# The front of a layer: key norms in pieces and later, bonus products a half later, PSUM banks of their own, three factor steps a block

## The chip, the cores and the metric

The kernel runs on one core of a Trainium2 chip. The metric is the device time of one execution in microseconds (us). TensorE (PE), VectorE (DVE), ScalarE (ACT), GpSimd (POOL) and SyncE (SP, which issues all the DMAs here) each work through their own queue in order and wait for each other by semaphores. PE's loads of weights are listed as PEld.

## What is computed

A block of gated delta rule and dilated attention with its feed-forward net is followed by two layers of a second kind. Each of those projects 1280 tokens (256 of context, 1024 of grid) by a wide matrix and feeds three mixers: a bidirectional RWKV recurrence, grouped-query attention and neighbourhood attention. The change is in the projection for the RWKV part and in the factors that the recurrence takes from it:

```
u = _centred_conv3(u, conv_w)                     # conv over 3 tokens, 1280 channels
r, k, v, dd, ad = split(u)                        # 3 x 384 channels, 2 x 64 of low rank
decay = exp(-exp(-softplus(-(w0 + tanh(dd) @ w2)) - 0.5))      # for two directions
iclr  = sigmoid(a0 + ad @ a2)
kk    = k * k_k, divided by its norm in each head of 64
kd    = k * (1 + (iclr - 1) * k_a)
bonus = sum over a head of (r * (kd_forward + kd_backward) * r_k), times v
```

## The kernel before

`front` (L2318) runs once for each of the two layers, between the block before it and `stage`, where recurrence and attention run. It has three parts, in this order: `project`, `project_att` and `project_na`. A generator, `factors`, is advanced step by step from the first two (`next(side, None)`).

**Order.** In the front, instructions are not placed by hand. The program gives their priority; a scheduler that simulates the engines puts each engine's queue in a fixed order at build time, and an engine that would be idle in this simulation takes later work that is ready. Tiles of one tag share `bufs` slots, and a new tile has to wait until a slot is released. When a pool is closed, the next one takes over its memory, and a tile waits for the tiles that it overlaps. PSUM banks are different: the eight `[128, 512]` banks are single tiles, `K.bank` hands them out by tag and turn (L103), and whoever gets a bank waits, in program order, for the one that had it before. `DENSE` gives banks 0 and 1 to "mm" (dense products), 2 and 3 to "a" (transposes), and 4, 5 and 6 to "r", which norms, transposes of the attention part and factors share. Bank 7 is not used there.

**`project`** (L1377) goes through ten blocks of 128 columns. `Dense.load` brings weights and splits them into a high and a low part; `Dense.chan` (L251) makes, for each of three token segments (256, 512, 512), a chain of 24 products (L243 to L245) into an "mm" bank, and `k.copy` evicts it into `raw`, on ACT (L129) and DVE (L133) in turn. Then the convolution (L1407 to L1409, DVE) writes `cv`. Block 0 holds the hidden layers of the low-rank parts; blocks 1 to 9 are r, k, v of three pairs of heads. Every block is stored in `R`. After a k block (2, 5, 8) follows the key norm: squares into `sq` (L1433, L1434, ACT), sums by `heads_rsqrt_bc` (products L1356, a copy L1358, power of -1/2 on POOL L1361, spread by products L1372), and four multiplications into `kn`, which is the tile of `raw` (L1440), stored by L1444. After a v block (3, 6, 9) ten transposes (L1425) are evicted into `vt` by `k.copy` and stored by twelve small DMAs (L1430). `raw`, `cv` and `sq` share the tag "t5" with four slots. From block 4 on, four steps of `factors` follow each block.

**`factors`** (L1548) treats each of three pairs in two halves of 640 tokens, in five steps a half, 30 in all. A half loads r, k, `kn` and v as one tile `X` (L1567). For each of two directions it makes four small products from the hidden layers (L1577, two for each of two kinds), with tanh evictions on ACT (L1579), then a scan, exponentials and products on DVE, ACT and POOL, and stores `bk` (L1606) and `G` (L1610). At the end `kd` of both directions is summed (L1613, POOL), multiplied (L1614, DVE), summed over a head by PE (L1617) and multiplied into v in place (L1618), which is stored as `vb` (L1619).

**`project_att`** (L1451) makes v for attention token tile by token tile (`nv`, L1464), turns the rest of v, and makes q and k with their norms (`qk_norm`). Its tiles lie in a pool that takes over the memory of `project`'s. `project_na` follows with dense products only.

Of the kernel before, what the change touches and what calls it, by code (L numbers as in the profile page):

```python
# [22 lines left out]
DENSE = {"mm": FULL[0] + FULL[1], "a": FULL[2] + FULL[3], "r": FULL[4] + FULL[5] + FULL[6]}  # L23
FINISH = {"mm": FULL[0] + FULL[1] + FULL[5] + FULL[7], "r": FULL[6] + FULL[2] + FULL[3]}
# [1275 lines left out]
NT = 1280  # L1300
# [77 lines left out]
def project(k, I, l, last, hp, dn, hT, L, side):  # L1378
# [5 lines left out]
    def slot(nm):  # L1384
        return hp.tile([128, 1284], F32, tag="t5", name=nm, bufs=4)


    w = None
    for j in range(10):
# [11 lines left out]
        def ev(p, t0, n):  # L1401
            o = t0 + (1 if t0 < CTX else 3)
            k.copy(raw[:, o:o + n], p)
        dn.chan(w, j % 2 * 128, hT, segs, ev)
        a = slot("cv")
# [9 lines left out]
        else:  # L1415
# [4 lines left out]
            if kind == 2:  # L1420
                for b0, m in ((0, 4), (4, 4), (8, 2)):
                    p = k.bank([128, 4, 128], "a")
                    for i in range(m):
                        o = (b0 + i) * 128 + (0 if b0 + i < 2 else 2)
                        nc.tensor.transpose(p[:, i], a[:, o:o + 128], k.ident)  # L1425
                    vt = hp.tile([128, 2, 4, 64], F32, tag="vt", name="vt", bufs=2)
                    k.copy(vt[:, :, :m], p[:, :m].rearrange("p b (h v) -> p h b v", h=2))
                    for c in range(2):
                        for h in range(2):
                            nc.sync.dma_start(L.vT[:, pr, h, b0 * 2 + c:(b0 + m) * 2:2], vt[c * 64:c * 64 + 64, h, :m])  # L1430
            if kind == 1:
# [3 lines left out]
                kn = raw  # L1435
                for b0, m, p in heads_rsqrt_bc(k, hp, sq, 0, NT, 1.0, "max", 1e-12):

                    for b in ((b0, 2), (b0 + 2, 2)) if b0 == 0 else ((b0, m),):
                        o = b[0] * 128 + (0 if b[0] < 2 else 2)
                        nc.vector.scalar_tensor_tensor(  # L1440
                            kn[:, b[0] * 128:(b[0] + b[1]) * 128].rearrange("p (b t) -> p b t", t=128),
                            a[:, o:o + b[1] * 128].rearrange("p (b t) -> p b t", t=128), L.kk[:, pr:pr + 1],
                            p[:, b[0] - b0:b[0] - b0 + b[1]], ALU.mult, ALU.mult)
                nc.sync.dma_start(L.R[:, pr * 4 + 2, :], kn[:, 0:1280])  # L1444
        if j > 3:
            for _ in range(4):
                next(side, None)

# [98 lines left out]
def factors(k, I, l, wk, L):  # L1547
# [13 lines left out]
    nc.sync.dma_start(hid, L.R[:, 12])  # L1561
    for pr in range(3):
        for a in range(0, NT, N):
            tk = slice(a, a + N)
            pc = slice(pr, pr + 1)
            X = t1("X4", (128, 4, N))
            nc.sync.dma_start(X, L.R[:, pr * 4:pr * 4 + 4, tk])  # L1567
            r, kx, kk, v = (X[:, i] for i in range(4))
            r3, kk3 = (x.rearrange("p (c t) -> p c t", t=64) for x in (r, kk))
            kds = []  # L1570
            for d in range(2):
                th = [t1("th0"), t1("th1")]
                for kind in range(2):
                    for x in range(0, N, 320):
                        p = k.bank([128, 320], "r")
# [4 lines left out]
                                             bias=L.w0[:, kind * 2 + d, pc])  # L1580
                yield
# [33 lines left out]
            for x in range(0, N, 320):  # L1615
                p = k.bank([128, 320], "r")
                nc.tensor.matmul(p, lhsT=k.c("same"), rhs=b[:, x:x + 320], start=True, stop=True)  # L1617
                nc.vector.tensor_tensor(v[:, x:x + 320], v[:, x:x + 320], p, ALU.mult)  # L1618
            nc.sync.dma_start(L.vb[:, pr, tk], v)  # L1619
            yield  # L1620

# [695 lines left out]
def front(k, tc, I, l, last, dn, hT, L, dp):  # L2317

    nc = k.nc
    for nm, shape in (("R", [128, 13, NT]), ("vT", [64, 3, 2, 20, 64]), ("nqk", [128, 4, NT]), ("gqk", [128, 4, NT]),  # L2320
                      ("nv", [128, 10, 384]), ("gates", [128, 8, NT]), ("ydr", [128, 8, NT]), ("bk", [128, 3, 2, 2, NT]),
                      ("G", [128, 3, 2, 20, 128]), ("vb", [128, 3, NT])):
        setattr(L, nm, dp.tile(shape, F32, tag=nm + "d", name=f"{nm}{l}", bufs=1))
    pool = lambda name: tc.tile_pool(name=f"{name}{l}", bufs=1, reuse_waits="tile", side="left")
# [230 lines left out]
```

## Time and profile before

| | us |
|---|---|
| median of three runs | 4414.95 |
| the three runs | 4407.27, 4414.95, 4433.86 |
| the profiled execution | 4414.57 |
| its span | 4412.8 |

The profile is of one execution; its times are counted from the start of the span. The front of layer 0 lies at about 1666 to 2084, that of layer 1 at about 3101 to 3507. "Busy" is time in which an engine executes; matmuls are pipelined, so a row's duration is longer than the distance to the next one. The granted clock of PE is given as a share of 2.4 GHz; 0.5 is 1.2 GHz. Of a row of the timeline, the bracket at its end tells the idle time of the engine just before it and what ended it.

### The profile page before, as it was taken

What the parts mean: (1) busy time and instruction counts of PE and PEld (TensorE: products, weight loads), DVE (VectorE), ACT (ScalarE), POOL (GpSimd) and SP (SyncE); (2) the same over time, 40 slices, a digit from 0 to 9 for tenths busy, and PEclk for the clock granted to TensorE, in tenths of its full rate; (3) what the DMA queues carried; (4) which work ended last, traced back from release to release, by engine and by line L of the source; (5) the groups of instructions that cost most, each with busy time, mean ns of one, the idle gap of its engine ahead of it and who ended that gap; (6) DMA issues with size and microseconds to landing.
All of it is one profiled execution on the core that took longest, in us unless ns stands there. A gap on an engine that the chain in (4) does not pass through costs nothing. (4 is left out here: it accounts for less than half of the span.)

```text
span 4412.8 us, 91628 instructions
## 1 busy us (share of the span) xinstructions
PE 3949.0 (89%) x36914; PEld 3200.0 (73%) x36914; DVE 2166.8 (49%) x4701; ACT 1448.3 (33%) x2831; POOL 1699.5 (39%) x3201
## 2 busy tenths in 40 slices
PE   8989998989999989899869898988989987898878
PEld 6767777967888867578747776778767866676658
DVE  5633332499221155664235555557566424554546
ACT  4244443321111132221125554442222114554341
POOL 2444333433232254342223444336444224434424
PEclk9999999999999989889979999999889998999889
DMA  3343224354111133453232334354345333324434
GB/s 112 117 131 88 82 74 131 127 162 151 44 46 50 43 120 114 152 179 95 81 102 63 74 73 109 91 157 144 114 156 177 104 98 81 76 64 100 100 111 138
DMA packets 523961, 466.87 MB, mean 106 GB/s; under 512 B 66416, under 2 KB 448656, under 8 KB 523408
## 3 DMA queue, kind: packets, MB, share of 16 engines
q1 hardware_dynamic: 523536, 461.02, 35.7%
q8 instruction: 289, 4.73, 0.4%
q14 instruction: 136, 1.11, 0.1%
HBM read 330.43 MB, written 130.43 MB: 104 GB/s over the span
## 5 line engine op out<-in xcount | busy, mean ns | idle before, releaser
L154 POOL TENSOR_TENSOR wlo<-wraw,whi 128x1024 fp32r<-128x1024 f32 (+3 forms) x134 | 318.9, 2395 | 565.1 <-ACT whi L153 513.1
L436 POOL TENSOR_TENSOR wY<-wR,wX 128x60 f32<-128x60 f32 (+5 forms) x900 | 233.3, 259 | 405.2 <-DMA wR<-wD 353.0
L153 ACT CAST whi<-wraw 128x1024 fp32r<-128x1024 f32 (+3 forms) x164 | 156.9, 989 | 372.5 <-PE bank L245 162.8
L691 DVE CUSTOM_DVE_ANT_0 S<-bank,zero 128x256 f32<-128x256 f32 (+1 forms) x372 | 204.5, 558 | 151.4 <-PE bank L687 149.4
L245 PE MATMUL bank<-h2T,wlo 128*128 128x512 f32 x704 | 278.5, 397 | 0.0
L244 PE MATMUL bank<-h2T,whi 128*128 128x512 f32 x704 | 278.0, 395 | 0.0
L243 PE MATMUL bank<-h2T,whi 128*128 128x512 f32 x704 | 275.6, 394 | 0.3 <-ACT h2T L785 0.3
L727 ACT COPY PT<-bank 128x512 f32<-128x512 f32 x346 | 201.7, 584 | 222.4 <-PE bank L723 221.6
L243 PE MATMUL bank<-whi,yh 128*128 128x256 f32 x832 | 240.5, 289 | 31.7 <-ACT yh L153 31.7
L438 POOL TENSOR_TENSOR wX<-wX,wY 128x60 f32<-128x60 f32 (+5 forms) x900 | 239.1, 266 | 70.5
L723 PE MATMUL bank<-cst,S 128*128 128x128 f32 x1416 | 238.4, 292 | 23.5 <-ACT PT L727 14.6
L744 PE MATMUL bank<-PT,nav 128*64 128x128 f32 (+1 forms) x2832 | 242.8, 294 | 16.5 <-ACT PT L727 16.1
L245 PE MATMUL bank<-whi,yl 128*128 128x256 f32 x832 | 238.9, 288 | 0.5 <-POOL yl L154 0.5
L244 PE MATMUL bank<-wlo,yh 128*128 128x256 f32 x832 | 239.2, 288 | 0.0
L744 PEld LDWEIGHTS bank<-PT,nav 128*64 128x64 f32 (+1 forms) x2832 | 154.4, 141 | 86.8 <-issue 55.3
L415 POOL TENSOR_TENSOR wB<-A,cst 128x256 f32<-128x256 f32 x60 | 45.2, 753 | 446.6 <-DVE A L1889 446.5
L723 PEld LDWEIGHTS bank<-cst,S 128*128 128x128 f32 x1416 | 164.1, 146 | 62.8 <-ACT PT L727 26.2
L648 ACT ACTIVATE S<-S,mx 128x1280 f32<-128x1280 f32 (+3 forms) x180 | 202.7, 1127 | 9.1 <-DVE mx L695 6.4
L243 PE MATMUL bank<-hT,whi 128*128 128x512 f32 x464 | 190.4, 410 | 9.1 <-ACT sqkv L131 6.7
L244 PE MATMUL bank<-hT,whi 128*128 128x512 f32 x464 | 187.3, 404 | 0.0
L243 PEld LDWEIGHTS bank<-whi,yh 128*128 128x128 f32 x832 | 162.5, 195 | 33.2 <-ACT yh L153 32.9
L245 PE MATMUL bank<-hT,wlo 128*128 128x512 f32 x464 | 186.2, 402 | 0.0
(467 smaller groups left out, 10919.3 us busy)
## 6 DMA issues: line engine op xcount, KB each, us to landing
wraw<-in_w_in SPq DMA_DIRECT2D x86, 512.0 KB
wR<-wD SPq DMA_DIRECT2D x60, 512.0 KB
wm<-in_w_mod SPq DMA_DIRECT2D x96, 256.0 KB
X<-R SPq DMA_DIRECT2D x12, 1280.0 KB
G<-gt SPq DMA_DIRECT2D x24, 640.0 KB
bk<-bk SPq DMA_DIRECT2D x24, 640.0 KB
bk<-bk SPq DMA_DIRECT2D x120, 128.0 KB
G<-G SPq DMA_DIRECT2D x240, 64.0 KB
```

The source lines that it names most:

```text
L153: self.nc.scalar.copy(hi, raw)
L154: (eng or self.nc.gpsimd).tensor_tensor(lo, raw, hi.bitcast(F32), ALU.subtract)
L243: nc.tensor.matmul(p, lhsT=lh, rhs=rh, start=kk == 0, stop=False)
L244: nc.tensor.matmul(p, lhsT=lh, rhs=rl, start=False, stop=False)
L245: nc.tensor.matmul(p, lhsT=ll, rhs=rh, start=False, stop=kk == n - 1)
L436: eng.tensor_tensor(t, custom(R, i * 64 + i + 1, [((15 - 2 * i) * 64 + 31 - i, 2), (16, 2), (1, n)]), custom(x, i, [(47 - 2 * i, 2), (16, ...
L438: eng.tensor_tensor(o, o, t, ALU.subtract)
L648: nc.scalar.activation(s[:, :total], s[:, :total], AF.Exp, bias=mx[:, 5:6], accum_out=mx[:, 6:7])
L691: nc.vector.tensor_tensor_reduce(out=s[:, c0:c0 + n], in0=p[:, c0 % 512:c0 % 512 + n], in1=b, scale=1.0, scalar=-3.0e38, op0=ALU.add, op1= ...
L723: nc.tensor.transpose(pt[:rows[i], i], P[h][0][:, c0:c0 + rows[i]], k.ident)
L727: nc.scalar.copy(t[:, :full], pt[:, :full])
L744: nc.tensor.matmul(pv[h * 64:h * 64 + 64, 0], lhsT=V, rhs=t[:V.shape[0], i], start=seen[h] == 1, stop=seen[h] == n)
```

## The change

- `front` sets `FRONT`: "mm" and "a" as before, "r" on banks 4 and 5, and a new tag "f" on banks 6 and 7, which all products of `factors` use.
- The tag "t5" has five slots.
- The key norm is a generator, `unit`. Its first `next` comes right after the squares and does nothing; the second comes after the dense products of the next block and does sums, copy and power; the third comes after the dense products of the block after that, or after the loop for block 8, and does the spreading products, the four multiplications and the store. The result goes into `sq` itself, not into `raw`.
- Evictions into `raw` and `vt` are all on ACT.
- Three steps of `factors` follow a block, in place of four.
- In `factors`, v is loaded into a tile `X1` of its own (two slots), the other three into `X3`. The bonus (products, multiplication, store) of a half is kept in `late` and done in the next half, right after the factor products of its first direction; the last one is done at the end.

```diff
+FRONT = {"mm": FULL[0] + FULL[1], "a": FULL[2] + FULL[3], "r": FULL[4] + FULL[5], "f": FULL[6] + FULL[7]}
 ...
-        return hp.tile([128, 1284], F32, tag="t5", name=nm, bufs=4)
+        return hp.tile([128, 1284], F32, tag="t5", name=nm, bufs=5)
+
+    def unit(pr, a, sq):
+
+        yield
+        norms = heads_rsqrt_bc(k, hp, sq, 0, NT, 1.0, "max", 1e-12, slow=True)
+        next(norms)
+        yield
+        for b0, m, p in norms:
+
+            for b in ((b0, 2), (b0 + 2, 2)) if b0 == 0 else ((b0, m),):
+                o = b[0] * 128 + (0 if b[0] < 2 else 2)
+                nc.vector.scalar_tensor_tensor(
+                    sq[:, b[0] * 128:(b[0] + b[1]) * 128].rearrange("p (b t) -> p b t", t=128),
+                    a[:, o:o + b[1] * 128].rearrange("p (b t) -> p b t", t=128), L.kk[:, pr:pr + 1],
+                    p[:, b[0] - b0:b[0] - b0 + b[1]], ALU.mult, ALU.mult)
+        nc.sync.dma_start(L.R[:, pr * 4 + 2, :], sq[:, 0:1280])
 ...
-    w = None
+    w, norm = None, iter(())
     for j in range(10):
 ...
-            k.copy(raw[:, o:o + n], p)
+            nc.scalar.copy(raw[:, o:o + n], p)
         dn.chan(w, j % 2 * 128, hT, segs, ev)
+        next(norm, None)
 ...
-                    k.copy(vt[:, :, :m], p[:, :m].rearrange("p b (h v) -> p h b v", h=2))
+                    nc.scalar.copy(vt[:, :, :m], p[:, :m].rearrange("p b (h v) -> p h b v", h=2))
 ...
-                kn = raw
-                for b0, m, p in heads_rsqrt_bc(k, hp, sq, 0, NT, 1.0, "max", 1e-12):
-                    ...
-                nc.sync.dma_start(L.R[:, pr * 4 + 2, :], kn[:, 0:1280])
+                norm = unit(pr, a, sq)
+                next(norm)
         if j > 3:
-            for _ in range(4):
+            for _ in range(3):
                 next(side, None)
+    next(norm, None)
 ...
+    def bonus(pr, tk, b, v):
+        for x in range(0, N, 320):
+            p = k.bank([128, 320], "f")
+            nc.tensor.matmul(p, lhsT=k.c("same"), rhs=b[:, x:x + 320], start=True, stop=True)
+            nc.vector.tensor_tensor(v[:, x:x + 320], v[:, x:x + 320], p, ALU.mult)
+        nc.sync.dma_start(L.vb[:, pr, tk], v)
+
+    late = None
 ...
-            X = t1("X4", (128, 4, N))
-            nc.sync.dma_start(X, L.R[:, pr * 4:pr * 4 + 4, tk])
-            r, kx, kk, v = (X[:, i] for i in range(4))
+            X, v = t1("X3", (128, 3, N)), t1("X1", bufs=2)
+            nc.sync.dma_start(X, L.R[:, pr * 4:pr * 4 + 3, tk])
+            nc.sync.dma_start(v, L.R[:, pr * 4 + 3, tk])
+            r, kx, kk = (X[:, i] for i in range(3))
 ...
-                        p = k.bank([128, 320], "r")
+                        p = k.bank([128, 320], "f")
 ...
+                if late:
+                    bonus(*late)
+                    late = None
                 yield
 ...
-            for x in range(0, N, 320):
-                ...
-            nc.sync.dma_start(L.vb[:, pr, tk], v)
+            late = pr, tk, b, v
             yield
+    bonus(*late)
 ...
+    k.places = FRONT
```

## Rows read from the trace of the kernel before

**Rows 1.** The page, busy time of each engine and its share of the span.

```profile
PE 3949.0 (89%) x36914; PEld 3200.0 (73%) x36914; DVE 2166.8 (49%) x4701; ACT 1448.3 (33%) x2831; POOL 1699.5 (39%) x3201
```

**Rows 2.** Stretches: length, busy PE, PEld, DVE, ACT, POOL (instructions), PE clock, DMA.

```profile
1666.00:1846.00 180.00, 171.90 (x890) 134.49 (x890) 107.98 (x94) 44.45 (x71) 63.61 (x64) 0.97 0.38 130
1850.70:1894.50 43.80, 23.56 (x99) 15.07 (x100) 27.18 (x31) 13.15 (x23) 25.16 (x16) 0.62 0.55 195
1896.00:2084.00 188.00, 179.49 (x1119) 157.05 (x1119) 100.25 (x127) 42.22 (x71) 69.61 (x85) 0.96 0.41 127
3287.60:3327.80 40.20, 22.91 (x98) 14.98 (x99) 25.57 (x29) 10.30 (x18) 22.47 (x15) 0.63 0.52 185
```

**Rows 3.** Timeline of PE, layer 0: start, us, line, operands, count, idle before.

```profile
1839.84 0.40 PE L244 MATMUL bank<-hA,whi 128*128 128x512 f32 x1
1840.08 0.39 PE L245 MATMUL bank<-hA,wlo 128*128 128x512 f32 x1
...
1850.23 0.28 PE L244 MATMUL bank<-wlo,hA 128*128 128x256 f32 x1
1850.35 0.28 PE L245 MATMUL bank<-whi,hA 128*128 128x256 f32 x1
...
1860.04 2.50 PE L1617 MATMUL bank<-kd,cst 128*128 128x320 f32 x4 [5.66 <-DVE kd L1614]
...
1864.52 4.43 PE L1356 MATMUL bank<-cst,sq 128*128 128x2 f32 x20
...
1894.60 0.88 PE L243 MATMUL bank<-whi,hA 128*128 128x256 f32 x1
```

**Rows 4.** PE's groups in 1850.7 to 1894.5: busy, mean ns, idle before, releaser.

```profile
L1577 PE MATMUL bank<-hid,w2s 32*128 32x320 f32 x22 | 9.9, 606 | 7.1 <-ACT th L1579 7.1
L1617 PE MATMUL bank<-kd,cst 128*128 128x320 f32 x7 | 4.5, 787 | 7.2 <-DVE kd L1614 7.2
...
L1372 PE MATMUL bank<-cst,hrs 128*64 128x128 f32 x40 | 3.8, 375 | 6.1 <-POOL hrs L1361 6.1
```

**Rows 5.** PE's waits, first two layer 0, last layer 1: total, times, longest.

```profile
PE bank L1617 <- DVE kd L1614: 11.0, 4, 5.7
PE bank L243 <- DVE raw L133: 7.1, 2, 5.7
...
PE bank L1356 <- ACT sq L1433: 5.4, 1, 5.4
```

**Rows 6.** Timeline of ACT, layer 0.

```profile
1816.33 0.94 ACT L1579 ACTIVATE th<-bank,w 128x320 f32<-128x320 f32 x2 [5.59 <-DVE bk L1604]
...
1831.53 1.14 ACT L1434 ACTIVATE sq<-cv,kk 128x1024 f32<-128x1024 f32 x1
...
1889.25 0.53 ACT L1579 ACTIVATE th<-bank,w 128x320 f32<-128x320 f32 x1 [2.87 <-DVE bk L1604]
1889.67 0.36 ACT L129 COPY nv<-bank 128x256 f32<-128x256 f32 x1
```

**Rows 7.** Timeline of DVE, layer 0.

```profile
1845.84 0.68 DVE L133 COPY raw<-bank 128x512 f32<-128x512 f32 x1
...
1859.10 0.89 DVE L1614 SCALAR_TENSOR_TENSOR kd<-X,rk,kd 128x640 f32<-128x640 f32 x1 [2.91 <-POOL kd L1613]
...
1869.08 0.88 DVE L1407 TENSOR_SCALAR cv<-raw,conv 128x1282 f32<-128x1282 f32 x1
```

**Rows 8.** Both fronts, by tile: count, then ns min/median/max, first and last start.

```profile
L133 DVE COPY raw<-bank x30: 400/677/692, 1666.4 to 3281.2; 128x512 f32<-128x512 f32 x20, 128x256 f32<-128x256 f32 x10
L129 ACT COPY raw<-bank x27: 351/587/596, 1666.1 to 3273.0; 128x512 f32<-128x512 f32 x20, 128x256 f32<-128x256 f32 x7
...
L1408 DVE SCALAR_TENSOR_TENSOR cv<-raw,conv,cv x20: 1544/1555/3574, 1675.5 to 3302.9; 128x1282 f32<-128x1282 f32 x20
...
L1608 DVE TENSOR_TENSOR gt<-ec,X x24: 809/816/2193, 1744.7 to 3381.3; 128x640 f32<-128x640 f32 x24
```

**Rows 9.** Timeline of SP's queue, layer 0.

```profile
1880.69 7.73 SPq L1430 DMA_DIRECT2D vT<-vt  x10
```

More of the change, by code (lines that the diff above doesn't have):

```diff
@@ L1434, in project @@
                 nc.scalar.activation(sq[:, 256:1280], t, AF.Square, scale=L.kk[:, pr:pr + 1])
-                kn = raw
-                for b0, m, p in heads_rsqrt_bc(k, hp, sq, 0, NT, 1.0, "max", 1e-12):
[L1438 to L1443, printed above, removed]
-                nc.sync.dma_start(L.R[:, pr * 4 + 2, :], kn[:, 0:1280])
+                norm = unit(pr, a, sq)
+                next(norm)
         if j > 3:
-            for _ in range(4):
+            for _ in range(3):
                 next(side, None)
+    next(norm, None)
 def project_att(k, I, l, last, hp, dn, hT, L, side):
@@ L1614, in factors @@
             nc.vector.scalar_tensor_tensor(b, r, L.rk[:, pc], b, ALU.mult, ALU.mult)
-            for x in range(0, N, 320):
-                p = k.bank([128, 320], "r")
-                nc.tensor.matmul(p, lhsT=k.c("same"), rhs=b[:, x:x + 320], start=True, stop=True)
-                nc.vector.tensor_tensor(v[:, x:x + 320], v[:, x:x + 320], p, ALU.mult)
-            nc.sync.dma_start(L.vb[:, pr, tk], v)
+            late = pr, tk, b, v
             yield
+    bonus(*late)
 def qk_norm(k, wk, p, t, last, L):
```

## The prediction

> **What bounds the kernel now.** I read the page first, for the engine that sets the time: TensorE (PE) is busy for 89% of the span [rows 1]. A change of the front can therefore pay only where PE stands still or runs slowly inside it. Next come the stretches, for where that is. The front occurs once per layer. Before its middle and after it (layer 0), PE is busy for about 95% of the time at a granted clock of 0.96 to 0.97, that is, at 2.4 GHz nearly throughout. In the stretch where the ten column blocks have ended and the attention products should go on, it is busy for 23.6 of 43.8 us in layer 0 and 22.9 of 40.2 in layer 1, at a clock of 0.62 and 0.63: much of that at 1.2 GHz [rows 2].
>
> Then PE's timeline shows what this stretch is. The last product of the column blocks starts at 1840.08, and two token tiles of v follow until 1850.35 + 0.28 = 1850.63. The next dense product comes at 1894.60. That is a hole of 44.0 us [rows 3]; layer 1 has the same, of 40.2 us [rows 2]. Inside, PE does only small work, with 20.4 us of waits in layer 0: 7.1 for ScalarE (ACT) to empty factor banks, 7.2 for `kd` of L1614, 6.1 for the key norm [rows 4]. The waits over the whole front add what lies outside the hole: 7.1 for VectorE (DVE) to copy out a dense bank, and 11.0 - 7.2 = 3.8 more for L1614; in layer 1, 5.4 for the squares of a key norm, and L1614 again [rows 5].
>
> Why does dense work stop? Both "mm" banks hold finished v tiles, and their first eviction into `nv` runs at 1889.67 [rows 6]. `nv` takes over memory of the pool that `project` leaves, so it comes after the tail of the last column block. That tail is late for one reason: `raw` of block 9 was out of its bank at 1845.84 + 0.68, but its convolution L1407 starts at 1869.08, though DVE had idle time in between, 2.91 us in one piece [rows 7]. The four "t5" slots are then full (`raw`, which also becomes `kn`, `cv` and `sq` of block 8, `raw` of block 9), so `cv` of block 9 has none. `sq` is released when L1356 has read it, at 1864.52 + 4.43 = 1868.95, 0.13 us before the convolution [rows 3, 7]. `sq` itself was ready at 1831.53 + 1.14 [rows 6]. L1356 stands behind L1617 and L1577 on PE, because norms and factors rotate through the same three "r" banks in program order, and L1617 waited for L1614 [rows 3, 4].
>
> **The change part by part.**
>
> *Slots, banks, norms in pieces.* A fifth "t5" slot, norms alone on "r", factors alone on "f", and the norm's first piece after the next block's dense products: each removes a link of that chain. `cv` of block 9 has a slot at once. Writing the normalised keys into `sq` frees `raw` early. The new tail, counted from T = 1840.3, the end of the column blocks' dense work: eviction 0.6, convolution 0.9 + 1.55 + 1.55 = 4.0 (L1409 like L1408) [rows 7, 8], ten transposes and the first copies about 2 (estimate: forty products of L1372 with the same width took 3.8 at the low clock [rows 4]). So it is done at T + 7; if DVE is in factor operations, some us later. Twelve `vT` stores follow; ten take 7.73 us of SP's queue [rows 9], so all end near T + 16, landing not counted. PE's two v tiles take until T + 6 (48 products of 256 columns, 0.12 apart by the contiguous ones [rows 3]). The hole then ends between T + 7, if `nv` lies on a slot that is free early, and T + 20, if it lies on the last thing stored: 1 to 14 us of hole. I cannot tell which slot it is; DVE also has factor steps to do, so I take 13 per layer, near the upper end. 44.0 + 40.2 - 26 = 58 us gained.
>
> *Not all of it is gain.* The factor products in the hole (9.9 + 4.5 us, mostly at half clock [rows 4]) were done while nothing else could run. At 0.62 of the clock they amount to 8.9 us at the full one. With a third still in the new hole, 6 per layer return between dense products: +12.
>
> *Evictions on ACT.* A full eviction on DVE (L133) took 0.68 us, on ACT (L129) 0.59 [rows 8], so the copy itself gains nothing that PE sees. What it removes is the place behind the convolution on DVE: 7.1 us in layer 0 [rows 5]. ACT gets 57 evictions instead of 27 of them [rows 8]; 30 x 0.59 is 18 us over two layers on an engine that is busy for 44 of 180 us [rows 2], hidden as long as nothing late stands ahead of them (a rival below).
>
> *Bonus a half later.* L1617 no longer waits for a fresh `kd`; the work is unchanged. Outside the hole this is worth 3.8 us in layer 0, and I take the same for layer 1. `v` in a tile of its own lets the next X load leave without waiting for the `vb` store; its cover is the factor chain, which is off PE's path. These waits sum to 7.1 + 3.8 + 5.4 + 3.8 = 20; I count three quarters, 15, because the order on each engine is fixed ahead and some will reappear elsewhere.
>
> *Three steps a block.* 18 of 30 steps run beside the column blocks instead of 24. Six per layer move beside the attention products, where DVE is busy for 100 of 188 us [rows 2]. They have to be finished before the next stage reads G and bk, and dense work of over 100 us still lies ahead of that, so their end is covered. Their DVE operations can delay the reads of a dense bank. Six steps are 2.4 directions, with three two-input operations each: 7 operations per layer, which take 0.82 us or up to 2.19 [rows 8]. If every one is late and exposed: 7 x 1.4 = 10 us per layer; if none, 0. I take a third: +7.
>
> The Trainium skill, "SBUF — State Buffer", section "Who interferes with whom", says that a DVE instruction with two SBUF inputs and a GpSimd instruction that reads SBUF exclude each other, and the later one waits for the whole of the other. The spread of L1608 agrees, and by that rule the 10 us would all be there beside the attention's GpSimd work: 4361 would become about 4374.
>
> *Sum* against the profiled execution, 4414.57 us (span 4412.8, 1.8 around it; the median of the three runs, 4414.95, is 0.4 higher): -58 + 12 - 15 + 7 = -54, so 4361 us.
>
> **Rivals.**
>
> 1. *All of it goes.* Waits of 20.4 and the half clock (23.6 us busy x 0.38 = 9) per layer, some 59 in all, and the 20 elsewhere: 4414.6 - 79 = 4336. For it: `nv` may lie on a slot that is free early. Against it: the tail of 7 us is longer than the two v tiles.
> 2. *The change does in part what happens anyway.* Instructions are placed by a simulated order, and the engine that is free takes later work. If `nv` stays behind the stores and the factors, the hole shrinks to 28 us: -28 + 6 (half of the returned work) - 7.5 (half of the waits) + 7 = -22.5 gives 4392. For it: ACT's first `nv` copy stood directly behind an L1579 that waited for DVE [rows 6]. Against it: that tail began 23 us late.
> 3. *Attention is crowded.* All 20 us of the moved steps are exposed, in place of 7: 4374, or 4382 if half of the other waits stay too.
> 4. *Slower: ACT holds up the banks.* L1579 waited 5.59 us for DVE's L1604 [rows 6], and every raw eviction now queues on ACT. PE fills the other bank in 24 products of 0.24 [rows 3], about 5.7 us, so a wait up to that is free; beyond it, each us is PE's. At double the wait, 11.2, in each of the 12 blocks that have factor steps, 12 x 5.5 = 66: 4427. It decides for slower from 10.2 us a block (54 / 12 + 5.7, rounded), and reaches 1% at 13.8.
>
> **How the numbers follow.** Forecast 0.50, with its own range 4340 to 4382 (a hole of 4 to 22 us per layer is 18 to either side, and 3 more for the other waits); rival 1: 0.12; rival 2: 0.22; rival 3: 0.08; rival 4: 0.08. A measurement of this kernel tells about 1% from no change, that is, below 4371 or above 4459. Three quarters of the forecast and all of rival 1 lie below 4371: 0.50. Rival 4 beyond 13.8 us a block: 0.05. The rest is 0.45. The range of 8 in 10 runs from rival 1 to past rival 2, with 16 us for what stands at its side: 4336 to 4408.
>
> **What would show it.** In the new profile, right: the convolution of block 9 starts within some 3 us of its last eviction; L1356 for block 8 lies between dense products of block 9; the hole before the first dense product after the v tiles is 4 to 20 us, and the clock of that stretch is over 0.85; no PE wait for `kd` at L1617. Wrong: `nv` evicted over 20 us after the v tiles; PE waits at L243 for ACT's `raw`, or for `xg` in the attention products by more than 10 us per layer; a stretch outside the two fronts that differs by more than some us, which would be a cause that I have not counted.

## The result, and the profile after

The changed kernel takes 4373.8 us (median of 4 runs, 4363.1 to 4383.5) against 4419.8 us (4 runs of the kernel before beside it, 4407.3 to 4433.9). The ratio is 0.9895, with a 95% interval of 0.9868 to 0.9923: 46 us less. The profiled run took 4363.1 us, with a span of 4361.3. The forecast was 4361, with a range of 4336 to 4408.

Where the 51.5 us between the two spans come from is best seen by stretch. "Front" is here from the first dense product of the column blocks to the last dense product of the attention part.

| stretch, us | before | after | difference |
|---|---|---|---|
| layer 0, ten column blocks | 174.0 | 183.0 | +9.0 |
| layer 0, rest of the front | 243.0 | 212.8 | -30.2 |
| layer 1, ten column blocks | 179.0 | 181.7 | +2.7 |
| layer 1, rest of the front | 227.4 | 205.4 | -22.0 |
| all that lies outside the two fronts | 3589.4 | 3578.4 | -11.0 |

So the fronts gave 40.5 us. The rows of the two fronts, from the view of stretches (length, busy PE, PEld, DVE, ACT, POOL with their instructions, PE clock, DMA), first of before:

```profile
1666.50:2083.47 416.97, 379.98 (x2134) 310.62 (x2135) 239.93 (x255) 100.51 (x164) 159.25 (x166) 0.93 0.42 137
3100.96:3507.40 406.44, 374.49 (x2018) 302.53 (x2019) 241.05 (x252) 99.27 (x162) 161.39 (x168) 0.92 0.43 139
```

and of after:

```profile
1667.95:2063.74 395.79, 375.36 (x2134) 310.69 (x2135) 219.74 (x229) 112.64 (x186) 161.45 (x168) 0.95 0.44 144
3081.90:3469.00 387.10, 362.78 (x2029) 297.40 (x2030) 225.87 (x226) 110.94 (x180) 162.48 (x168) 0.95 0.45 146
```

PE's idle time in the fronts (length less busy) fell from 37.0 + 31.9 to 20.4 + 24.3 us, which is 24.2. Its busy time fell from 754.5 to 738.1, which is 16.3, for the same work at a clock of 0.95 in place of 0.92 to 0.93: less of it is done at 1.2 GHz. The two add up to the 40.5.

The hole itself shrank, but not to the size forecast. The stretches of after that answer to [rows 2]:

```profile
1667.95:1850.90 182.95, 173.17 (x876) 137.56 (x877) 100.49 (x83) 56.09 (x94) 70.84 (x71) 0.94 0.42 140
1853.60:1881.10 27.50, 22.67 (x123) 15.20 (x122) 23.82 (x25) 11.23 (x22) 18.95 (x11) 0.81 0.70 232
1881.10:2063.70 182.60, 176.78 (x1120) 155.85 (x1120) 94.13 (x121) 43.51 (x69) 70.24 (x86) 0.97 0.43 133
```

The last column product of layer 0 ends at 1850.9, v tiles run from 1853.6 to 1861.4 and from 1867.1 to 1870.6, and dense work resumes for good at 1881.1: two gaps of 5.7 and 10.5 us in place of one of 44.0 [rows 3]. In layer 1 the gaps are 2.4, 5.1 and 14.8 us in place of 40.3. In the timeline of PE, 6 of the 20 norm sums of block 8 now lie between dense products of block 9 and 14 right behind its last one, and the last gap ends on ACT's eviction into `nv`:

```profile
1844.47 0.73 PE L1357 MATMUL bank<-cst,sq 128*128 128x2 f32 x6
1850.76 1.62 PE L1357 MATMUL bank<-cst,sq 128*128 128x2 f32 x14
...
1881.14 0.58 PE L244 MATMUL bank<-whi,hA 128*128 128x256 f32 x1 [3.06 <-ACT nv L130]
```

Against the gain stands a new stop inside the column blocks. PE's waits of after, layer 0 (total, times, longest):

```profile
PE bank L1357 <- ACT sq L1451: 7.3, 1, 7.3
PE bank L1597 <- ACT th L1599: 3.4, 3, 1.6
PE bank L244 <- ACT nv L130: 3.1, 1, 3.1
```

The 11.0 us for `kd` and the 7.1 us for DVE's `raw` of [rows 5] are gone from layer 0. In their place PE stands 7.3 us at the norm sums, for the squares of block 5. In layer 1 it stands there for 6.5 us (before it had waited 5.4 us for squares), and 6.4 of its 10.0 us for `kd` are left. With the products around it, dense work stops for 13.1 us at 1771.9 and for 12.2 in layer 1, where before it stopped for 5.7 and 9.9. The timelines of DVE, of ACT and of PE show why:

```profile
1764.42 2.40 DVE L1425 TENSOR_SCALAR cv<-raw,conv 128x1282 f32<-128x1282 f32 x1 [0.46 <-ACT raw L1420]
1766.73 3.00 DVE L1627 SCALAR_TENSOR_TENSOR th<-th,X 128x640 f32<-128x640 f32 x1
1769.65 2.85 DVE L1426 SCALAR_TENSOR_TENSOR cv<-raw,conv,cv 128x1282 f32<-128x1282 f32 x1
...
1778.29 1.54 DVE L1427 SCALAR_TENSOR_TENSOR cv<-raw,conv,cv 128x1282 f32<-128x1282 f32 x1
```

```profile
1778.46 0.53 ACT L1599 ACTIVATE th<-bank,w 128x320 f32<-128x320 f32 x1 [11.18 <-DVE bk L1628]
1779.87 0.51 ACT L1451 ACTIVATE sq<-cv,kk 128x256 f32<-128x256 f32 x1 [0.88 <-DVE cv L1427]
1780.29 1.13 ACT L1452 ACTIVATE sq<-cv,kk 128x1024 f32<-128x1024 f32 x1
1781.33 0.83 ACT L1420 COPY raw<-bank 128x256 f32<-128x256 f32 x2
```

```profile
1780.43 4.61 PE L1357 MATMUL bank<-cst,sq 128*128 128x2 f32 x20 [7.31 <-ACT sq L1451]
```

The convolution of block 5 takes from 1764.4 to 1779.8 on DVE, because factor operations stand between its three parts. Its squares follow at once, and the norm sums, which stand in PE's queue ahead of more dense work, wait for them. Two full `raw` banks wait on ACT meanwhile, behind a tanh that waited 11.18 us for DVE.

### The profile page after: what moved, and what is told of

It reads as the page before. It is cut to its first block, busy times and chain, and to the rows that moved or that the text cites. A ratio compares the mean times of both kernels' runs of the same rounds, so it can differ in the third digit from the quotient of the medians.

```text
span 4361.3 us, 91613 instructions
## 1 busy us (share of the span) xinstructions
PE 3925.0 (90%) x36914; PEld 3189.2 (73%) x36914; DVE 2137.5 (49%) x4664; ACT 1470.8 (34%) x2868; POOL 1701.1 (39%) x3201
## 5 line engine op out<-in xcount | busy, mean ns | idle before, releaser
L724 PE MATMUL bank<-cst,S 128*128 128x128 f32 x1416 | 234.0, 288 | 20.0 <-ACT PT L728 11.8
```

The lines of the kernel that those rows point to most:

```text
L724: nc.tensor.transpose(pt[:rows[i], i], P[h][0][:, c0:c0 + rows[i]], k.ident)
```

## The experiments

The table holds, for each kernel, the largest stop of dense work beside the norm of block 5 (layer 0 / layer 1), the gaps of 5 us and more between the end of the blocks and the resumed dense work, the sum of both fronts and the time outside them in its profiled execution, all from PE's timeline, and the measured ratio to the kernel before with its interval.

| kernel | stop in the blocks | hole | fronts | outside | ratio |
|---|---|---|---|---|---|
| before | 5.7 / 9.9 | 44.0 / 40.3 | 823.4 | 3589.4 | 1 |
| before, 5 slots | 4.5 / 9.9 | 37.3 / 32.1 | 816.3 | 3599.9 | 0.9991 [0.9972, 1.001] |
| before, 5 slots, own banks | 7.1 / 5.2 | 16.1 / 14.8 | 801.1 | 3587.3 | 0.9937 [0.9914, 0.9961] |
| before, 3 steps | 4.1 / 9.9 | 20.6 / 18.7 | 805.5 | 3576.9 | 0.9945 [0.9921, 0.9968] |
| before, nv elsewhere | 4.1 / 9.9 | none here (see text) | 830.0 | 3591.2 | 1.002 [0.9997, 1.0043] |
| after | 13.1 / 12.2 | 5.7+10.5 / 5.1+14.8 | 782.9 | 3578.4 | 0.9895 [0.9868, 0.9923] |
| after, 4 slots | 14.4 / 12.3 | 7.3+10.6 / 5.7+13.9 | 778.4 | 3585.0 | 0.9869 [0.9837, 0.9901] |
| after, shared banks | 9.8 / 13.3 | 19.9 / 19.9 | 785.2 | 3586.1 | 0.9898 [0.9869, 0.9927] |
| after, evictions shared | 8.5 / 14.1 | 5.8+11.8 / 6.6+11.5 | 783.2 | 3574.8 | 0.9889 [0.9859, 0.9919] |
| after, bonus in its own half | 12.6 / 14.1 | 18.3 / 14.3 | 794.1 | 3579.7 | 0.9911 [0.9878, 0.9943] |
| after, norms in one go | 5.6 / 11.6 | 15.8 / 15.8 | 775.0 | 3571.6 | 0.9844 [0.9814, 0.9873] |
| after, norms in one go, 4 steps | 7.0 / 12.4 | 21.6 / 10.8+8.6 | 807.2 | 3574.9 | 0.9939 [0.9913, 0.9964] |
| after, norms in one go, nv elsewhere | 5.2 / 12.4 | none (3.1 / 3.1) | 751.9 | 3603.0 | 0.9883 [0.9845, 0.992] |
| after, norms in one go, nv elsewhere, th1 in two tiles | 5.5 / 10.5 | none (3.1 / 3.1) | 753.5 | 3593.9 | 0.9844 [0.9804, 0.9883] |

Outside the fronts no edit acts, and yet that time lies between 3571.6 and 3603.0 us. A difference of some 20 us between two of these kernels is therefore read from the fronts first, and from the ratio only with that in mind.

**1. The slot alone, and the slot with the banks.** The prediction put the hole down to a missing "t5" slot. The first run gives the kernel before that slot and nothing else:

```
-        return hp.tile([128, 1284], F32, tag="t5", name=nm, bufs=4)
+        return hp.tile([128, 1284], F32, tag="t5", name=nm, bufs=5)
```

> The kernel before with a fifth t5 slot and nothing else. Theory of the chain (cv of block 9 waits for the slot of sq, and sq for the norm sums that stand behind the factors on PE): the convolution of block 9 starts within about 5 us of its last eviction, the holes after the v tiles shrink from 44.0 and 40.2 us to about 25 each, since the norm of block 8 still stands behind the factors; time 0.992 to 0.995 of before. Rival (the order of norms and evictions makes the hole, slots do not): both holes stay above 38 us and the time is that of before within 0.3%.

Measured: 0.9991, no change, as the rival has it; the hole is 37.3 and 32.1 us, between the two. Its timelines of DVE, of PE and of ACT:

```profile
1864.03 0.68 DVE L133 COPY raw<-bank 128x512 f32<-128x512 f32 x1
...
1866.51 0.88 DVE L1407 TENSOR_SCALAR cv<-raw,conv 128x1282 f32<-128x1282 f32 x1
```

```profile
1881.08 2.50 PE L1617 MATMUL bank<-kd,cst 128*128 128x320 f32 x4 [3.67 <-DVE kd L1614]
1883.52 2.08 PE L1577 MATMUL bank<-hid,w2s 32*128 32x320 f32 x4
1885.56 4.43 PE L1356 MATMUL bank<-cst,sq 128*128 128x2 f32 x20
```

```profile
1905.46 0.37 ACT L129 COPY nv<-bank 128x256 f32<-128x256 f32 x1
```

The convolution of block 9 now follows its last eviction after 1.8 us, where it came 22.6 us later before [rows 7]: the link through the slot was read rightly. But it wasn't the link that ends last. The norm sums of block 8 still stand behind the factors' bonus products on PE, which wait for `kd`, and `nv` is evicted only 15.5 us after their end. The second run adds the banks of their own ("r" for norms, "f" for factors; `FRONT` and the same line of the bonus products are left out here):

```
+    k.places = FRONT
-                        p = k.bank([128, 320], "r")
+                        p = k.bank([128, 320], "f")
```

> The kernel before with the fifth slot and the bank split (norms on r with 4 and 5, factors on f with 6 and 7); norms in one go, evictions, bonus and four steps as before. Theory of the chain: slot and banks are the two links, so the holes are those of the changed kernel, 15 to 22 us, and the time is 0.988 to 0.992 of before. Rival (the later norms or the evictions on ACT carry the gain): holes of 25 us or more, time over 0.993.

Measured: 0.9937. The hole falls to 16.1 and 14.8 us, 53.4 us less in all, but the fronts lose only 22.3 of 823.4 us. In layer 0 nothing is gained: its blocks take 192.8 us in place of 174.0, with 52 factor products before the first v tile in place of 42. In layer 1 the blocks take 171.8 in place of 179.0. So in one layer what left the hole returned inside the blocks; why the two layers differ wasn't found.

**2. Three steps a block.** The kernel before with this one edit, with slots and banks as they were:

```
-            for _ in range(4):
+            for _ in range(3):
                 next(side, None)
```

> The kernel before with three factor steps after a block in place of four, and nothing else. Theory of the queue (the norm of block 8 takes its r banks, in program order, after the factor steps that precede it: with four steps a block that is step 16, with three it is step 12, which is long done on the chip): the norm sums of block 8 run between dense products of block 9, sq is free early, cv of block 9 has its slot although there are four, and the holes shrink from 44.0 and 40.2 us to 15 to 25; time 0.989 to 0.993 of before. Rival (fewer steps only move work; slots and banks are what makes the hole): holes over 35 us, time over 0.997.

Measured: 0.9945, as much as slot and banks together and a smaller gain than the first theory's 0.989 to 0.993; the holes are 20.6 and 18.7 us, as it said. In its timeline of PE the norm sums of block 8 lie among the dense products of block 9, 23 us earlier than in [rows 3], in 2.29 us in place of 4.43:

```profile
1841.33 2.29 PE L1356 MATMUL bank<-cst,sq 128*128 128x2 f32 x20
```

The slots are still four and the banks still shared. With fewer factor steps ahead of it in program order, the norm gets its turn early, and the slot comes free of itself. The holes are 45.0 us shorter and the fronts only 17.9, since the steps have moved: of the 96 factor products of a layer, as the trace lists them, 42 now lie behind the resumed dense work in place of 26, and this stretch takes 200.3 and 196.8 us in place of 188.9 and 179.5. The view of stretches for the factor products alone (length, busy PE with their number, PE clock, DMA), layer 1, first before, then this kernel:

```profile
3327.87:3507.40 179.53, 10.41 (x26) 0.98 0.43 134
```

```profile
3283.40:3480.18 196.78, 14.69 (x42) 0.96 0.45 144
```

The opposite run takes the changed kernel with norms in one go (experiment 4) and gives it four steps back:

```
-            for _ in range(3):
+            for _ in range(4):
                 next(side, None)
```

> The changed kernel with each key norm in one go, and with four factor steps a block again: of the change, the later bonus, the banks, the slot and the evictions on ScalarE are left. Theory A (three steps instead of four carry a large part: fewer factor operations stand before the tail of block 9): each hole is 25 to 32 us instead of 16, ratio 0.989 to 0.993. Theory B (banks of their own and the fifth slot carry it, and the number of steps only moves work): the holes stay at 14 to 19 us, ratio 0.983 to 0.986.

Measured: 0.9939 against 0.9844 with three steps. The fronts are 32.2 us longer, which is two thirds of the 48.4 that the kernel with three steps gains on before. The holes are 21.6 and 19.4 us in place of 15.8 each, between the two theories. But the loss lies ahead of them: up to the first v tile the blocks take 34.7 us more over two layers, with 68 and 64 factor products in them in place of 52 each, and at a lower clock. The stretches up to the first v tile, first of the kernel with three steps, then of this one:

```profile
1660.42:1842.30 181.88, 176.66 (x892) 138.52 (x893) 101.55 (x86) 56.28 (x95) 75.69 (x74) 0.96 0.43 149
3070.43:3251.00 180.57, 172.55 (x820) 133.35 (x820) 98.78 (x84) 54.60 (x90) 71.62 (x74) 0.92 0.44 151
```

```profile
1666.45:1864.30 197.85, 190.97 (x944) 146.00 (x944) 118.03 (x102) 64.91 (x110) 85.00 (x82) 0.94 0.44 150
3080.98:3280.30 199.32, 187.18 (x836) 140.54 (x837) 113.14 (x95) 60.45 (x102) 80.97 (x80) 0.89 0.44 148
```

The end of the hole of layer 0, on PE, is a wait for factor banks:

```profile
1888.34 2.50 PE L1598 MATMUL bank<-hid,w2s 32*128 32x320 f32 x4 [8.80 <-ACT th L1600]
1891.82 1.43 PE L1598 MATMUL bank<-hid,w2s 32*128 32x320 f32 x2 [0.98 <-ACT th L1600]
1894.40 0.58 PE L244 MATMUL bank<-whi,hA 128*128 128x256 f32 x1 [1.15 <-DVE nv L134]
```

So among the parts that were undone one at a time (here and in experiments 3 and 4) the steps are the largest, and added alone to the kernel before they bring as much as slot and banks together. Banks, evictions and the later bonus were not added to it alone.

**3. Other parts undone in the changed kernel.** Four runs undo one part each. The slot:

```
-        return hp.tile([128, 1284], F32, tag="t5", name=nm, bufs=5)
+        return hp.tile([128, 1284], F32, tag="t5", name=nm, bufs=4)
```

> The changed kernel with four t5 slots. Theory of the chain: sq and cv of a k block now live two blocks longer, so four slots are fewer than what is alive; the column blocks themselves wait for slots, and the holes come back to 30 us or more; time 0.997 to 1.010 of before. Rival (banks, norms in pieces and evictions do the work without the slot): time within 0.3% of the changed kernel, about 0.990.

Measured: 0.9869, fronts 778.4 against 782.9. The fifth slot isn't needed beside the rest of the change. That `raw` is free as soon as it is convolved, with the normalised keys written into `sq`, may be the reason; no run shows it. The banks (factors and norms on the same three again, the bonus products too):

```
-    k.places = FRONT
-            p = k.bank([128, 320], "f")
+            p = k.bank([128, 320], "r")
```

> The changed kernel with the banks of before: norms, turns and factors share r with 4, 5 and 6. Theory of the chain: the norm sums of block 8 again stand behind factor products on PE, holes of 25 to 32 us instead of 16 and 20, time 0.993 to 0.997 of before. Rival (the slot alone is enough, since cv no longer needs what the norm holds): holes under 22 us, time 0.988 to 0.991.

Measured: 0.9898, fronts 785.2, holes of 19.9 us. The 2.3 us are within what one profile can tell. Slot and banks were not undone together, so each may stand in for the other. The evictions, given to whichever of the two engines the kernel's own balance picks:

```
-            nc.scalar.copy(raw[:, o:o + n], p)
+            k.copy(raw[:, o:o + n], p)
```

(and the same for `vt`).

> The changed kernel with evictions of raw and vt on ACT and DVE in turn, as before. Theory: they carry nothing of the gain; in block 6, where an eviction stands 11.2 us behind a factor eviction on ACT and PE stops for 13.1 and 12.2 us, half of the evictions get away from it, so the stop shrinks or moves: time 0.986 to 0.992 of before. Rival (a copy on DVE stands behind the convolution and the factors): waits of PE for DVE's raw of 5 to 10 us per layer come back, time 0.992 to 0.996.

Measured: 0.9889, fronts 783.2, as after. The stop at block 5 goes from 13.1 / 12.2 to 8.5 / 14.1 us. In layer 0 it is now the wait that the rival names, though not its time. PE's waits of the blocks there:

```profile
PE bank L244 <- DVE raw L134: 8.5, 1, 8.5
```

DVE's copy of `raw` stands right behind the last part of block 5's convolution (1773.58, after 1772.11 + 1.54). The bonus products back in their own half (the call at the end goes too):

```
-            late = pr, tk, b, v
+            bonus(pr, tk, b, v)
```

> The changed kernel with the bonus products at the end of their own half, as before. Theory: PE waits for the fresh kd again, 2 to 6 us at some of the six halves per layer, 8 to 20 us in all: time 0.991 to 0.995 of before. Rival (with fewer steps and banks of their own these waits are covered by dense products): waits of PE for kd under 4 us per layer, time within 0.2% of the changed kernel's 0.9895.

Measured: 0.9911, fronts 794.1. The ratio doesn't tell it from after; the fronts are 11.2 us longer, 4.1 in layer 0 and 7.1 in layer 1, by one profile of each. But that is not the wait which the later bonus was to remove: PE waits for `kd` by 2.8 and 1.2 us here, and by 0 and 6.4 in after. The rival is right on this wait and on the time, and what the 11.2 us come from isn't shown; the waits for squares and `raw` are longer, 27.8 us in place of 19.4 over both layers.

**4. Norms in one go.** The changed kernel, but each norm runs through behind its squares, as in the kernel before; `sq` still takes the result:

```
                 norm = unit(pr, a, sq)
-                next(norm)
+                for _ in norm:
+                    pass
```

> The changed kernel with each key norm in one go right after its squares, as before (the result still goes into sq). Theory of the queue: the order on the engines is made from readiness, so the pieces themselves bring little: front within 8 us of the changed kernel's 783 us (both layers), time 0.986 to 0.992 of before; the wait of PE for the squares of block 5 (7.3 and 6.5 us) changes place or goes. Rival (the later norms are what closes the hole): holes of 25 us or more in both layers, time 0.994 or more.

Measured: 0.9844, 4348.2 us: the pieces bring nothing and seem to cost time, though the intervals of the two ratios touch. The fronts are 7.9 us shorter than after's, and the stop at block 5 in layer 0 is 5.6 us in place of 13.1. Its timelines of ACT and PE there:

```profile
1771.87 0.51 ACT L1451 ACTIVATE sq<-cv,kk 128x256 f32<-128x256 f32 x1 [7.85 <-DVE cv L1427]
```

```profile
1772.43 0.61 PE L1357 MATMUL bank<-cst,sq 128*128 128x2 f32 x4 [2.24 <-ACT sq L1451]
```

PE waits 2.24 us for the squares in place of 7.31. In this order DVE puts less between the parts of the convolution: the squares start 8.7 us after block 5's last eviction (1762.60 + 0.58), where in after they start 15.5 us behind it (1763.79 + 0.59). In layer 1 the stop stays (11.5 us). Of the 25.6 us between the two medians the fronts hold 7.9; another 6.8 lie outside them in the profiles, the kernel before itself was 2.2 us faster beside these runs (4417.6), and for the rest there is no profile.

**5. The memory of nv.** The last gap of after ends on ACT's `nv`. `nv` lies on memory that `project` leaves. Three runs put it in a pool that is open during the whole front (the line that hands `fp` to `L` is left out):

```
-        nv = hp.tile([128, 256], F32, tag="nv", name="nv", bufs=2)
+        nv = L.fp.tile([128, 256], F32, tag="nv", name="nv", bufs=2)
```

First the kernel before with that edit alone:

> The kernel before, with one edit: the two nv tiles of the attention products lie in a pool that is open during the whole front, not in memory that the projection of the blocks leaves. Theory A (nv's memory closes the chain: it comes free only after the tail of the last block, norms and factors included): dense products go on under that tail, each hole of the kernel before (44 and 40 us) falls under 10 us, some 65 us go, 12 come back as factor products between dense ones: ratio 0.986 to 0.990, as good as the whole change. Theory B (the engines are busy with the tail anyway, in the order of the program: VectorE stands before the convolution of block 9, ScalarE before a factor bank, so that no bank is emptied whatever its target): the holes stay over 25 us, ratio 0.995 to 1.000.

Measured: 1.002, and the first theory falls as far as time goes. The dense products do run on at 1850, but 92 us later PE stops for 20.2 and 10.2 us (19.3 and 10.8 in layer 1), and the fronts are 6.6 us longer. PE's groups between 1942 and 1981, with busy time, mean and idle time before:

```profile
L1577 PE MATMUL bank<-hid,w2s 32*128 32x320 f32 x14 | 8.8, 805 | 6.8 <-ACT th L1579 6.8
...
L1617 PE MATMUL bank<-kd,cst 128*128 128x320 f32 x8 | 5.0, 777 | 7.0 <-DVE kd L1614 7.0
```

It is the hole of [rows 4] again, with nearly the same waits (7.1 and 7.2 there), further on: 48 and 46 factor products lie behind the first two v tiles in place of 26. So in this kernel the hole covered a chain that PE otherwise waits for at another place. Then the kernel of experiment 4 with that edit:

> The changed kernel with each key norm in one go behind its squares (as in the earlier run of that edit, 0.9844), and the two nv tiles in the pool that is open during the whole front. Theory A (the 16 us that are left of each hole are the wait for the memory that the projection leaves): they fall to 5 us or less in each layer, 20 to 22 us less, 2 to 4 of them given back by products that return between dense ones: ratio 0.979 to 0.982. Theory B (ScalarE stands before a factor bank that waits for VectorE's bk, and so empties no bank): the 16 us stay within 3, ratio 0.983 to 0.986.

Measured: in the trace the first theory holds. The 15.8 us are gone in both layers (3.1 are left, filled with norm and factor products), and ACT empties the first v bank at 1869.34, 7.2 us after its first product (1862.17):

```profile
1869.34 0.37 ACT L130 COPY nv<-bank 128x256 f32<-128x256 f32 x1
```

The fronts are the shortest so far, 751.9 us with 11.1 and 12.0 us of idle PE and a clock of 0.97 to 0.98:

```profile
1681.94:2061.58 379.64, 368.58 (x2134) 305.00 (x2135) 217.86 (x229) 111.08 (x186) 161.75 (x168) 0.98 0.46 150
3082.41:3454.67 372.26, 360.22 (x2029) 295.17 (x2030) 214.21 (x226) 109.19 (x180) 155.99 (x168) 0.97 0.47 152
```

The time isn't: 0.9883, no better than after. What the fronts gained (23.1 us on experiment 4), the rest lost: 31.4 us, 21.5 of them ahead of layer 0's front, where the two programs give PE the same instructions in the same order. The stretch from 400 to 600 us, first in the kernel of experiment 4, then in this one:

```profile
400.00:600.00 200.00, 189.07 (x1579) 147.23 (x1578) 71.83 (x232) 84.75 (x183) 74.98 (x151) 0.99 0.30 85
```

```profile
400.00:600.00 200.00, 187.58 (x1485) 146.03 (x1485) 69.13 (x226) 83.20 (x176) 67.97 (x145) 0.92 0.26 74
```

PE is busy as long, at a granted clock of 0.92 in place of 0.99, and gets through 94 products fewer. The other layout isn't needed for such a difference: over the 14 profiles the time ahead of layer 0's front runs from 1660.4 to 1684.5 us, and the longest is that of the kernel before with five slots. What sets the clock there stays open. The last run adds a second tile for `th1`, so that ACT's tanh need not wait until DVE's `bk` has read the first:

```
-                th = [t1("th0"), t1("th1")]
+                th = [t1("th0"), t1("th1", bufs=2)]
```

> As the run with nv in the other pool, and th1, the second tanh of a factor step, in two tiles instead of one. Theory A (ScalarE's waits of 4 to 11 us before a factor bank, for VectorE's bk, which reads th1, hold up the dense banks behind them): the stop of PE during block 6 (5.6 and 11.6 us) and the rest of the hole fall by 8 to 12 us over two layers: ratio 0.002 to 0.003 under the run with nv alone. Theory B (VectorE, and not the tile, is late; ScalarE's wait moves to the next operation that needs VectorE): the two runs agree within 0.001.

Measured: 0.9844, 4344.9 us, the lowest median of all. The fronts are as without the edit (753.5 against 751.9), so the second theory is borne out by the trace: ACT's one long wait of layer 1 for `bk`, 10.4 us, is gone, and one of 11.4 us for DVE's scan (`c`) has come. Neither theory has the ratio. Of the 19 us between the medians the profiles show 9.1 outside the fronts, where the tile isn't used, and none inside; no cause for them was found.

The two lowest medians are thus those with norms in one go, 4348.2, and with `nv` and `th1` moved as well, 4344.9 us. The intervals of their ratios still touch that of after.

## Why the prediction came out as it did

The total was right: 4373.8 lies within the range, 12.8 us above the forecast, and at 1.05% on the edge of what a measurement tells. By its own steps less was right than the total says, and that the total came so close is in part luck. In the prediction's terms, as far as the two profiles can be split that way:

| term, us | forecast | profiles |
|---|---|---|
| hole and returned work (PE's idle time in the hole -23.7, its busy time in the fronts -16.3) | -58 + 12 | -40.0 |
| other waits (PE's idle time outside the hole) | -15 | -0.5 |
| moved steps | +7 | none moved |
| outside the fronts | 0 | -11.0 |

So the fronts gave 40.5 us in place of 54, and in these two profiles most of the difference is made up by the 11.0 outside them, which no edit touches.

- *The view of the hole: right.* What there was to gain lay where PE stood still behind the blocks, and the rest of the front of layer 0 lost 30.2 us, that of layer 1 22.0.
- *The link named as the cause: not the one that ends last.* "That tail is late for one reason" was wrong. The wait for the slot was there (convolution 1.8 us after its eviction once the slot is given), but the slot alone moved the time by a factor of 0.9991. Behind it stood the place of the norm in PE's queue, behind factor products that wait for DVE. The prediction had that line as the release of the slot, and a remedy for it in the banks, but not fewer factor steps.
- *The price of the edits: turned round.* Slots, banks and norms in pieces were to bring the 58 us, three steps were a cost of 7. Slot and banks alone do take 53.4 us off the holes, but 22.3 off the fronts: the work that leaves the hole costs far more elsewhere than the 12 us of the prediction. Undone one at a time in the changed kernel, slot and banks cost nothing that can be told (0.9869, 0.9898), and the norms in pieces bring nothing (0.9844 without them). The three steps alone bring 0.9945 to the kernel before and are worth 32 us of the fronts in the changed one with norms in one go.
- *The hole of 13 us: mis-sized.* It is 16.3 us in layer 0 and 22.2 in layer 1 with the short gap. 44.0 + 40.3 less these are 45.8 in place of 58. `nv` did lie on memory that comes late: with `nv` elsewhere (and norms in one go), 3.1 us are left. Counted from the end of the column products, 1850.9, the twelve vT stores run on SP from 12.9 to 21.1 us, where the forecast had 7 to 16, and ACT's first `nv` copy comes at 29.8, behind a tanh that waits 3.93 us for DVE's `bk`:

```profile
1879.88 0.94 ACT L1599 ACTIVATE th<-bank,w 128x320 f32<-128x320 f32 x2 [3.93 <-DVE bk L1628]
1880.71 0.37 ACT L130 COPY nv<-bank 128x256 f32<-128x256 f32 x1
```

- *Other waits, 15 us: nothing net.* This is the term that failed most plainly. Behind the resumed dense work the 3.8 us of waits for `kd` in each layer went as forecast, and PE's idle time there fell from 16.1 to 9.7 us (both layers). But in the blocks it rose from 13.8 to 19.7 us: the wait for `raw` went, and 7.3 and 6.5 us for the squares of block 5 came. Nor was it the later bonus that removed the waits for `kd`, since they stay away without it (2.8 and 1.2 us).
- *Moved steps, +7: in the changed kernel they did not move.* From the resumed dense work to the end of the front, layer 0 took 188.9 us before (1894.6 to 2083.5) and 182.6 after, layer 1 179.5 and 173.3, with the same dense products in it (1032 and 984, as the trace lists them) and 24 factor products per layer in place of 26. The other parts of the change bring factor work forward: 52 and 56 products lie before the first v tile in place of 42 and 46. The factor products alone, layer 0, first before, then after:

```profile
1894.60:2083.47 188.87, 10.25 (x26) 0.95 0.42 128
```

```profile
1881.14:2063.74 182.60, 8.82 (x24) 0.97 0.43 133
```

PE waits for `xg` by 1.9 and 1.4 us. So rival 3 didn't come, but not because moved steps are cheap: where they did move (three steps alone, experiment 2), the same stretch got 28.7 us longer over two layers, 9.7 of it idle time of PE.
- *The Trainium skill's price for it.* By "SBUF — State Buffer", section "Who interferes with whom", the sum had come to about 4374, and the median is 4373.8; that is a coincidence, since the stretch meant got shorter. The rule there says that a DVE instruction with two SBUF inputs waits for the whole of a GpSimd one that reads SBUF, when it comes second. The trace agrees, inside the blocks: L1426 of block 5 starts at 1769.65 and takes 2.85 us, against 1.55 in the median of its 20, and POOL reads SBUF until 1771.15. From there, 1.55 us would end at 1772.70; it ended at 1772.50:

```profile
1769.01 2.14 POOL L1625 TENSOR_TENSOR kd<-kd,X 128x640 f32<-128x640 f32 x1
```

- *Rival 4, ACT before the banks: there, but for few blocks.* In layer 0 ACT waits 8.62 us for DVE's `bk` until 1761.07, for which PE stands 1.6 + 0.8 us, and 11.18 us until 1778.46 with two `raw` banks behind it. With the evictions shared the stop is 8.5 us there, a wait for DVE's copy, and the fronts stay (783.2). DVE's long convolution of block 5, with factor operations between its parts, is the likelier cause, since squares and copy both stand behind it, and where it is shorter (norms in one go) so is the stop in layer 0. No run moves those factor operations alone, so this is argued, not shown.
- *What would show it.* The convolution of block 9 starts 2.0 us after its last eviction (1854.23 after 1851.68 + 0.58); L1357 lies between and right behind the dense products of block 9; no wait for `kd` in layer 0, but 6.4 us in layer 1; the clock of the hole is 0.81 and 0.86, where more than 0.85 was asked. The stretches outside the fronts differ by 11.0 us, 13.1 of it behind the second front (905.4 to 892.3): probably not the change's, since kernels that differ only in the fronts differ outside them by up to 31 us. Without these 11 us the profile gives 40.5, not the 54 forecast.

## What to carry to other kernels

A wait that is seen to end when a buffer comes free is proven to be the cause only when the buffer alone is given: here the slot moved its own wait by 20 us and the time by nothing, because the next link, a norm behind factor products in an in-order queue, ended almost as late. The Trainium skill, "Perfetto Trace Analysis", section "Optimization Strategy", has a repeated gap as a possible sign of too little SBUF or PSUM for the next tile. Here the same gap in both layers did end on such waits, but giving the slot alone (0.9991) or other memory for `nv` alone (1.002) brought nothing, and less side work ahead of it in program order did (0.9945). Where an engine's standstill covers a chain of side work, take work out of that chain's way or spread it before the standstill is removed, or it comes back at another point: with `nv` elsewhere alone, stops of 20.2 and 10.2 us came in place of 44.0; beside three steps, banks and slot no such stop came.

## What the runs showed of the hardware that was not expected

- The same PE instructions in the same order, ahead of everything that was edited, took 1660.4 us in one profile and 1681.9 in another, with granted clocks of 0.99 and 0.92 between 400 and 600 us. Over 19 runs the kernel before spread from 4391.9 to 4442.5 us. A difference of 23 us in the fronts was lost in this between two kernels of four runs each (0.9844 and 0.9883), while 17.9 and 22.3 us showed with ten and seven runs (0.9945, 0.9937).
- Twenty norm sums of 2 columns take 2.29 us between dense products, at a granted clock of 1.00, and 4.61 us behind a wait of 7.31, at 0.50: the standstill is paid a second time, at 1.2 GHz, by the work that follows it. In that stop of 13.1 us the granted clock is 0.62:

```profile
1771.90:1785.00 13.10, 5.77 (x25) 5.01 (x25) 10.28 (x9) 4.61 (x8) 5.92 (x7) 0.62 0.47 168
```
